# 18 of 22 feature tiles of each SwiGLU input projection in pairs through seven block products, with buffer pools opened and closed per sublayer

## The chip, the core and the metric

The kernel runs on one core of one Trainium2 chip. TensorE (PE) does the matmuls and writes to PSUM; VectorE (DVE), ScalarE (ACT) and GpSimd (POOL) do the elementwise work; each engine runs its own queue in program order and waits on semaphores. SyncE (SP) issues nearly all DMAs, in one queue. The metric is the device time of one execution in microseconds; lower is better. One execution was also profiled, and every row below is from that one.

## The reference: four layers of mixer and SwiGLU

There are 512 tokens of 1024 features in float32. Four layers each hold a token mixer (mLSTM, sliding-window attention, HGRN2, differential attention, in that order) and a SwiGLU channel mixer. Both are modulated by a conditioning vector and followed by a residual sum and a layer norm:

```python
FFN_HIDDEN = -(-8 * D_MODEL // (3 * 256)) * 256      # 2816
...
def swiglu(h, w_in, w_out):
    gu = h @ w_in
    return (jax.nn.silu(gu[..., :FFN_HIDDEN]) * gu[..., FFN_HIDDEN:]) @ w_out
...
    mod = jnp.einsum('bd,sde->sbe', cond, ada_w[i].astype(F32)) + ada_b[i][:, None, :].astype(F32)
    shift, scale, gate = jnp.split(mod.astype(x.dtype), 3, axis=-1)
...
    h = x * (1 + scale[1][:, None]) + shift[1][:, None]
    y = swiglu(h, ffn_w_in[i], ffn_w_out[i])
    x = layer_norm(DEEPNORM_ALPHA * x + (1 + gate[1][:, None]) * y.astype(x.dtype), ln_g[i, 1], ln_b[i, 1])
```

## The kernel before

Activations lie features by tokens: 128 partitions, 8 feature tiles (KD), 512 tokens. Every large matmul is done as three: both operands are split into a high part and a remainder, and `mm3` (L187 to L191) adds high x high (L189), low x high (L190) and high x low (L191) in PSUM. For the weights, `weights` (L170 to L185) loads a tile of up to 128 x 1024 into a `raw` buffer by DMA, ACT copies it to `wh` (L179), and DVE takes `wl` = raw - wh (L180). `raw` and `wp` (the pool of wh and wl) have five buffers each, so splits run ahead of PE by that much. The activations' high and low parts are `hh` (L424, ACT) and `hl` (L428, DVE, which subtracts hh from the POOL result `h` of L427); `modulate` makes the three per feature tile and token half.

The SwiGLU (`ffn`, L431 to L457) has 22 hidden feature tiles, each with a gate and an up projection: 8 k-tiles x 3 matmuls of 512 columns for each of the two, 48 a tile. The first two tiles run in two halves of 256 tokens, since the layer norm ahead delivers its halves one after the other. `gated` makes the activation of a tile: silu on ACT (L441), product on DVE (L442), the high copy on ACT (L443), the low part on DVE (L444). Tiles come in groups of 7, 7 and 8 (FGROUPS); after each group `out_proj` (L307 to L358) multiplies them into the 8 output rows and adds each to the residual (L326). In a sublayer's last group, rows 4 to 7 run in two token halves, A and B: layer norm (L361 to L411) of half 0 and its modulation run beside half B, and the next sublayer's input projection starts on half 0 when half B has been multiplied. The layer norm's rsqrt is a power on POOL (L487, `lnv`).

The conditioning (`ada`) is a matrix-vector product done by DVE: 24 columns for each of the 8 sublayers, 192 in all, each a load of 512 KB and one DVE instruction of 128x1024 (L113, with a short second row). They are kept in a list `todo`; each `weights` call pops `rate` of them.

Buffers: `big` (12) and `mid` (10) are pools for all sublayers, opened once in `__init__` (L47 to L57). A mixer's first buffers can therefore be written while the SwiGLU ahead still runs. Three such early writes matter here: the zeroed buffer of the sliding-window mixer (L700, POOL), the seven masks of HGRN (L944 to L949, five POOL instructions for each), and a load of the differential mixer's vectors on ACT's queue (L812). The order of the instructions comes from Python generators that `run` (L1128 to L1177) advances, and from a scheduler that places each instruction in its engine's queue by priority and readiness.

Of the kernel before, what the change touches and what calls it, by code (L numbers as in the profile page):

```python
# [19 lines left out]
P = 128  # L20
D = 1024
T = 512
KD = D // P
NTT = T // P
DEPTH = 4
HID = 2816
KF = HID // P
FGROUPS = (7, 7, 8)
# [13 lines left out]
class Trunk:  # L42
    rate, hold = 1, 0

    def __init__(self, ctx, tc, a, out):
        self.tc, self.nc, self.a, self.out = tc, tc.nc, a, out
        pool = lambda name, bufs, **k: ctx.enter_context(tc.tile_pool(name=name, bufs=bufs, **k))  # L47
        self.const = pool("const", 1)
        self.state = pool("state", 1)
        self.raw = pool("raw", 5)  # L50
        self.wp = pool("wp", 5)
        self.big = pool("big", 12)
        self.mid = pool("mid", 10)
# [63 lines left out]
    def ada_begin(self, sub, js=range(24)):  # L117
        mod = self.adap.tile([P, 24], F32, tag="mod", name=self.nm("mod"), bufs=3)
        self.todo += [lambda j=j: self.ada_column(mod, sub, j) for j in js]
# [21 lines left out]
    def first_input(self, sub, gate):
        nc, gp, V = self.nc, self.nc.gpsimd, self.nc.vector
        mod = self.ada_begin(sub, ())
# [22 lines left out]
        self.todo += [lambda j=j: self.ada_column(mod, sub, j) for j in range(16, 24)]  # L166
        self.todo.append(lambda: gp.tensor_scalar(gate, mod[:, 16:24], 1.0, None, ALU.add))
# [193 lines left out]
    def layer_norm(self, sub, nxt, half):  # L361
        nc = self.nc
        V = nc.vector
        t = slice(half * 256, half * 256 + 256)

        ps = self.bank()
# [6 lines left out]
        s, v = (self.lnp.tile([P, 2], F32, tag=x, name=self.nm(x), bufs=2) for x in ("lns", "lnv"))  # L373
# [47 lines left out]
    def modulate(self, z, hs, hb, k, t, eng=None):  # L421
        nc = self.nc
        h = self.lnp.tile([P, T], F32, tag="h", name=self.nm("h"), bufs=2)[:, t]
# [6 lines left out]

    def ffn(self, layer, gate):  # L431
        nc, a = self.nc, self.a
        j0 = 0
        for gi, gn in enumerate(FGROUPS):
            acts = []

            def gated(pss):
                for pg, pu in zip(pss[::2], pss[1::2]):
                    act = self.b4([P, 2, T], F32R)
                    s = self.b2([P, T])  # L440
                    nc.scalar.activation(s, pg, AF.Silu)  # L441
                    nc.vector.tensor_tensor(s, pu, s, ALU.mult)  # L442
                    nc.scalar.activation(act[:, 0, :], s, AF.Copy)  # L443
                    nc.vector.tensor_tensor(act[:, 1, :], s, act[:, 0, :].bitcast(F32), ALU.subtract)  # L444
                    acts.append(act)

            j = j0
            while j < j0 + gn:
                m = 2 if (gi == 0 and j == 0) else 1
                srcs = [a["ffn_in"][layer, jj, :, x, :] for jj in range(j, j + m) for x in range(2)]  # L450
                yield from self.proj_cols(srcs, "t" if m == 2 else None, gated)
                j += m
            srcs = [a["ffn_out"][layer, d, :, j0 * P : (j0 + gn) * P] for d in range(KD)]
            if gi == len(FGROUPS) - 1:
                return srcs, 1, acts
            yield from self.out_proj(srcs, 1, acts, gate, False)
            j0 += gn  # L457
# [670 lines left out]
    def run(self, plan):  # L1128

        self.setup()  # L1130
        subs = [2 * l + (k == "ffn") for k, l in plan]
# [3 lines left out]
        for i, (kind, layer) in enumerate(plan):  # L1135
            more = i + 1 < len(plan)
            gate = mods[2] if i else gate
            gen = getattr(self, kind)(layer, gate)
# [10 lines left out]
            self.rate, self.hold = 2 if kind == "mlstm" else 1, 10 if kind == "ffn" else 0  # L1149
# [27 lines left out]
        self.run_all(ln)  # L1177

# [14 lines left out]
def host(inputs):  # L1193
# [10 lines left out]
    r["ffn_in"] = w.transpose(0, 4, 2, 3, 1, 5).reshape(DEPTH, KF, P, 2, D)  # L1204
# [63 lines left out]
```

## Time and profile before

| what | us |
|---|---|
| timed runs, median (lowest to highest of 3) | 2482.39 (2480.66 to 2485.26) |
| the profiled execution's own time | 2479.98 |
| its span, first to last instruction | 2478.0 |
| PE busy in the span | 2434.8 |
| DVE / ACT / POOL busy | 1427.7 / 917.0 / 469.2 |

The four SwiGLU sublayers take some 360 us each. A matmul's record is longer than the distance to the next one, since matmuls are pipelined; the start-to-start distance is what a matmul costs in a full stream. A row of the views reads: line of the kernel, engine, operation, output <- inputs by the program's names, partitions x elements, and count; then busy time and mean duration, and the idle time before, with what ended it.

### The profile page before, as it was taken

What the parts mean: (1) busy time and instruction counts of PE and PEld (TensorE: products, weight loads), DVE (VectorE), ACT (ScalarE), POOL (GpSimd) and SP (SyncE); (2) the same over time, 40 slices, a digit from 0 to 9 for tenths busy, and PEclk for the clock granted to TensorE, in tenths of its full rate; (3) what the DMA queues carried; (4) which work ended last, traced back from release to release, by engine and by line L of the source; (5) the groups of instructions that cost most, each with busy time, mean ns of one, the idle gap of its engine ahead of it and who ended that gap; (6) DMA issues with size and microseconds to landing.
All of it is one profiled execution on the core that took longest, in us unless ns stands there. A gap on an engine that the chain in (4) does not pass through costs nothing.

```text
span 2478.0 us, 34314 instructions
## 1 busy us (share of the span) xinstructions
PE 2434.8 (98%) x12920; PEld 2054.2 (83%) x12920; DVE 1427.7 (58%) x2745; ACT 917.0 (37%) x1685; POOL 469.2 (19%) x714
## 2 busy tenths in 40 slices
PE   7999999999999999999999999999999999999998
PEld 5778888888768888889888898888888888888887
DVE  6956765545687656546555576565365557433334
ACT  3534422233654422234433344222345554422223
POOL 5003100003334000105333340000052124000002
PEclk9999999999999999999999999999999999999999
DMA  8842466642211566632212215666322211333331
GB/s 299 282 150 78 152 215 188 199 147 69 77 52 52 187 204 196 203 111 69 86 60 69 70 60 188 203 199 201 113 67 86 66 57 48 104 102 93 102 94 35
DMA packets 93973, 311.94 MB, mean 126 GB/s; under 512 B 10736, under 2 KB 13168, under 8 KB 93808
## 3 DMA queue, kind: packets, MB, share of 16 engines
q1 hardware_dynamic: 92800, 309.43, 39.0%
q8 instruction: 101, 1.65, 0.3%
q14 instruction: 64, 0.52, 0.1%
q10 hardware_dynamic: 1008, 0.32, 0.1%
HBM read 307.62 MB, written 2.10 MB: 125 GB/s over the span
## 4 chain that ended last, share of the span: by engine, by line
PE 87%; DVE 7%; POOL 2%; ACT 1%; issue 1%; DMA 1%; ACTq 0%; POOLq 0%; DVEq 0%
PE ps L189 26%; PE ps L191 26%; PE ps L190 26%; DVE wl L180 1%; PE ps L876 1%; PE ps L1042 1%; DVE raw L113 1%; POOL h L427 1%; PE ps L738 1%; PE ps L1103 1%; PE ps L904 1%; DVE xz L394 1%; PE ps L769 1%; DVE xz L402 1%; DMA raw<-in_m_vo 1%
## 5 line engine op out<-in xcount | busy, mean ns | idle before, releaser
L179 ACT ACTIVATE wh<-raw 128x1024 fp32r<-128x1024 f32 (+1 forms) x395 | 410.7, 1043 | 1011.2 <-PE ps L190 607.1
L189 PE MATMUL ps<-hh,wh 128*128 128x512 f32 (+1 forms) x1768 | 655.6, 372 | 16.2 <-ACT wh L179 13.1
L191 PE MATMUL ps<-hh,wl 128*128 128x512 f32 (+1 forms) x1768 | 657.5, 372 | 3.0 <-DVE wl L180 2.9
L190 PE MATMUL ps<-hl,wh 128*128 128x512 f32 (+1 forms) x1768 | 656.0, 372 | 0.4
L180 DVE TENSOR_TENSOR wl<-raw,wh 128x1024 fp32r<-128x1024 f32 (+1 forms) x395 | 492.9, 1251 | 273.8 <-ACT wh L179 251.3
L189 PE MATMUL ps<-b,wh 128*128 128x512 f32 (+1 forms) x1216 | 425.9, 351 | 0.0
L190 PE MATMUL ps<-b,wh 128*128 128x512 f32 (+1 forms) x1216 | 419.2, 345 | 0.0
L191 PE MATMUL ps<-b,wl 128*128 128x512 f32 (+1 forms) x1216 | 418.9, 345 | 0.0
L189 PEld LDWEIGHTS ps<-hh,wh 128*128 128x128 f32 x1768 | 333.3, 189 | 73.0 <-ACT wh L179 13.1
L191 PEld LDWEIGHTS ps<-hh,wl 128*128 128x128 f32 x1768 | 334.1, 189 | 63.4 <-DVE wl L180 6.4
L190 PEld LDWEIGHTS ps<-hl,wh 128*128 128x128 f32 x1768 | 334.0, 189 | 58.9 <-DVE hl L428 1.3
L113 DVE CUSTOM_DVE_ANT_0 raw<-raw,cond,adab 128x1024 f32<-128x1024 f32 x192 | 247.9, 1296 | 216.4 <-DMA raw<-in_ada_w 216.3
L189 PEld LDWEIGHTS ps<-b,wh 128*128 128x128 f32 x1216 | 230.3, 189 | 29.5 <-issue 1.2
L190 PEld LDWEIGHTS ps<-b,wh 128*128 128x128 f32 x1216 | 230.4, 189 | 29.3 <-issue 2.0
L191 PEld LDWEIGHTS ps<-b,wl 128*128 128x128 f32 x1216 | 230.2, 189 | 27.7
L189 PE MATMUL ps<-wh,hh 128*128 128x512 f32 (+1 forms) x608 | 239.3, 395 | 2.2 <-ACT wh L179 1.2
L326 DVE SCALAR_TENSOR_TENSOR xz<-ps,gate,xz 128x512 f32<-128x512 f32 (+1 forms) x208 | 130.0, 626 | 181.2 <-PE ps L191 180.6
L190 PE MATMUL ps<-wl,hh 128*128 128x512 f32 (+1 forms) x608 | 221.4, 364 | 0.1
L191 PE MATMUL ps<-wh,hl 128*128 128x512 f32 (+1 forms) x608 | 221.3, 364 | 0.0
L442 DVE TENSOR_TENSOR b<-ps,b 128x512 f32<-128x512 f32 x88 | 60.3, 690 | 138.3 <-PE ps L191 135.5
L189 PEld LDWEIGHTS ps<-wh,hh 128*128 128x128 f32 x608 | 115.1, 189 | 23.1 <-issue 3.7
L190 PEld LDWEIGHTS ps<-wl,hh 128*128 128x128 f32 x608 | 115.0, 189 | 18.3 <-issue 2.2
(254 smaller groups left out, 2376.8 us busy)
## 6 DMA issues: line engine op xcount, KB each, us to landing
raw<-in_ada_w SPq DMA_DIRECT2D x192, 512.0 KB, 4.0
raw<-in_ffn_in SPq DMA_DIRECT2D x176, 512.0 KB, 3.7
raw<-in_ffn_out SPq DMA_DIRECT2D x64, 448.0 KB, 3.5
raw<-in_ffn_out SPq DMA_DIRECT2D x32, 512.0 KB, 3.6
raw<-in_m_vo SPq DMA_DIRECT2D x16, 512.0 KB, 4.9
raw<-in_h_qf SPq DMA_DIRECT2D x16, 512.0 KB, 3.3
raw<-in_h_ig SPq DMA_DIRECT2D x16, 512.0 KB, 3.9
raw<-in_d_qk SPq DMA_DIRECT2D x16, 512.0 KB, 3.9
```

Source lines behind the costliest of these rows:

```text
L113: self.nc.vector.tensor_tensor_reduce(w, w, self.cond, 1.0, self.adab[:, sub, j : j + 1], ALU.mult, ALU.add, mod[:, j : j + 1])
L179: nc.scalar.activation(hi[:, :n], raw[:, :n], AF.Copy)
L180: (eng or nc.vector).tensor_tensor(lo[:, :n], raw[:, :n], hi[:, :n].bitcast(F32), ALU.subtract)
L189: nc.tensor.matmul(ps, lhs[0], rhs[0], start=start, stop=False)
L190: nc.tensor.matmul(ps, lhs[0], rhs[1], start=False, stop=False)
L191: nc.tensor.matmul(ps, lhs[1], rhs[0], start=False, stop=stop)
L326: nc.vector.scalar_tensor_tensor(z, ps[:, t], gate[:, d : d + 1], z, ALU.mult, ALU.add)
L394: V.tensor_tensor(z, z, st[:, 0, :], ALU.subtract)
L402: V.tensor_tensor(z, z, st[:, 1, :], ALU.mult)
L427: nc.gpsimd.tensor_scalar(h, z, hs[:, k : k + 1], hb[:, k : k + 1], ALU.mult, ALU.add)
L442: nc.vector.tensor_tensor(s, pu, s, ALU.mult)
L738: nc.tensor.matmul(ps, qTs[j][:, q], kz[:, :, k0 : k0 + nk * P], start=True, stop=True)
```

## The change

**Seven products.** Tiles 0 to 3 stay as they were. The other 18 tiles go in nine pairs a layer. For a pair, the weights form a 2 x 2 block matrix (gate and up; input features 0 to 511 and 512 to 1023; a block is two feature tiles of 128 by four k-tiles, 128 x 1024 in memory), and the activations form another (the two halves of the features; tokens 0 to 255 and 256 to 511). `strassen` forms the 2 x 2 product with seven block products instead of eight. A product is 2 x 4 x 3 = 24 matmuls of 256 columns; a pair has 168 of them, where there were 96 of 512 columns. The combinations of activation blocks (`t_forms`) are made and split once a layer, from the `h` tiles, which are now kept (`keep`) in four raw buffers until then. The combinations of weight blocks are made for each pair: DVE adds R3 += R2, R0 += R3, R3 = R0 - R2 and R1 += R0 in place, and each is split into high and low like any weight, so a pair has seven splits (four before) and four weight sums. Partial results are summed in PSUM banks and in ACT's copies of them. The next pair's first products are issued between the last ones of a pair.

**Order around it.** FGROUPS becomes (8, 8, 6). `rate` is 0 in the SwiGLU's input part, 2 in its first two output projections and 1 in the last; `hold` is 0. `ada_end` forces only the columns of its own sublayer.

**Pools.** `raw` gets seven buffers. `big`, `mid`, and the SwiGLU's `tf`, `pairs` and `mid` are opened at the start of each sublayer and closed at its end, in the same memory.

```diff
-FGROUPS = (7, 7, 8)
+FGROUPS = (8, 8, 6)
+FPLAIN = 4
...
+    def pools(self, kind):
+        if self.own:
+            self.own.close()
+        self.own = ExitStack()
+        pool = lambda name, bufs: self.own.enter_context(self.tc.tile_pool(name=self.nm(name), bufs=bufs))
+        if kind == "ffn":
+            self.tf, self.pairs, self.mid = pool("tf", 4), pool("pairs", 4), pool("mid", 7)
+        else:
+            self.big, self.mid = pool("big", 12), pool("mid", 10)
...
+    def t_forms(self):
+        nc, V = self.nc, self.nc.vector
+        b11, b12, b21, b22 = (self.keep[x] for x in ((0, 0), (0, 1), (1, 0), (1, 1)))
+        V.tensor_tensor(b11, b11, b12, ALU.subtract)
+        V.tensor_tensor(b12, b22, b12, ALU.subtract)
+        V.scalar_tensor_tensor(b22, b11, -1.0, b22, ALU.mult, ALU.subtract)
+        V.scalar_tensor_tensor(b21, b22, -1.0, b21, ALU.mult, ALU.subtract)
...
+        for i, r in ((6, b22), (5, b11), (7, b12), (4, b21)):
+            f = self.tf.tile([P, 2, 4, 256], F32R, tag="tf", name=self.nm("tf"))
+            nc.scalar.activation(f[:, 0], r, AF.Copy)
+            V.tensor_tensor(f[:, 1], r, f[:, 0].bitcast(F32), ALU.subtract)
+            forms[i] = [f[:, 0], f[:, 1]]
...
+        def product(ps, w, i, first):
+            for j in range(2):
+                for k in range(4):
+                    c = slice(j * 512 + k * P, j * 512 + k * P + P)
+                    m = [x[:, k, :] for x in forms[i]]
+                    for a, b in ((0, 0), (0, 1), (1, 0)):
+                        nc.tensor.matmul(
+                            ps[:, j * 256 : j * 256 + 256],
+                            w[a][:, c],
+                            m[b],
...
+        product(b2, w, 1, True)
+        p1 = copy(b2)
...
+        product(b1, w, 2, True)
+        add(p1, b1, p1)
+        nc.scalar.activation(p1, p1, AF.Silu)
+        yield
+        load(2)
+        load(3)
+        add(R[3], R[3], R[2])
+        add(R[0], R[0], R[3])
+        w = self.split(R[0])
+        product(b2, w, 6, False)
+        u2 = copy(b2)
+        yield
+        w = self.split(R[3])
+        b3 = self.bank()
+        product(b3, w, 5, True)
+        yield
+        V.tensor_tensor(R[3], R[0], R[2], ALU.subtract)
+        w = self.split(R[3])
+        product(b2, w, 7, False)
+        u3 = copy(b2)
+        add(u3, b3, u3)
+        yield
+        w = self.split(R[2])
+        product(b2, w, 4, False)
...
+        gated(0, p1, b2)
+        yield
+        add(R[1], R[1], R[0])
+        w = self.split(R[1])
+        product(b3, w, 3, False)
+        add(u2, b3, u2)
+        nc.scalar.activation(u2, u2, AF.Silu)
+        gated(1, u2, u3)
+        yield
...
+        for i in range(n):
+            g, act = steps[i]
+            for s in range(5):
+                if s == 3:
+                    begin(i + 1)
+                if s == 4 and i + 1 < n:
+                    next(steps[i + 1][0])
+                next(g)
+                yield 0.0
```

How the queues move is seen at three places. The first is DVE in the middle of a SwiGLU's input part. Before, a tile's rows and two columns of the conditioning alternate (`b` is an activation buffer, `wl` the weights' low part):

```order
L442 TENSOR_TENSOR b_402_2456<-ps_2406,b_402_2456 128x512 [waits PE_49]
L113 ISA raw_2612,mod_2086<-raw_2612,cond,adab 128x1024 [waits DMAHW7_49,DVE_49]
L113 ISA mod_2086 128x1
L444 TENSOR_TENSOR b_401_2455<-b_402_2456,b_401_2455 128x512 [waits Activation_49]
L180 TENSOR_TENSOR wl_2600<-raw_2597,wh_2599 128x1024 [waits DMAHW4_49]
L113 ISA raw_2677,mod_2086<-raw_2677,cond,adab 128x1024 [waits DMAHW1_49]
L113 ISA mod_2086 128x1
L180 TENSOR_TENSOR wl_2609<-raw_2606,wh_2608 128x1024 [waits DMAHW6_49,PE_49,Activation_49]
```

With the change, about half of one pair's rows in the same queue (L516 are sums of weights or of PSUM with a buffer, L480 splits, L542 the difference R0 - R2, L554 the gated product, L556 its low part):

```order
L480 TENSOR_TENSOR wl_3797<-raw_3533,wh_3796 128x1024 [waits PE_49,Activation_49]
L480 TENSOR_TENSOR wl_3836<-raw_3698,wh_3835 128x1024 [waits PE_49,Activation_49]
L516 TENSOR_TENSOR b_551_3694<-ps_3640,b_551_3694 128x512 [waits Activation_49]
L480 TENSOR_TENSOR wl_3866<-raw_3831,wh_3865 128x1024 [waits PE_49,Activation_49]
L542 TENSOR_TENSOR raw_3831<-raw_3698,raw_3829 128x1024 [waits DVE_49]
L554 SCALAR_TENSOR_TENSOR b_532_3500<-ps_3475,b_532_3500 128x512 [waits PE_49]
L480 TENSOR_TENSOR wl_3896<-raw_3831,wh_3895 128x1024 [waits Activation_49]
L556 TENSOR_TENSOR pair_3468<-b_532_3500,pair_3468 128x2x256 [waits Activation_49]
L516 TENSOR_TENSOR b_557_3729<-ps_3768,b_557_3729 128x512 [waits PE_49]
L480 TENSOR_TENSOR wl_3930<-raw_3927,wh_3929 128x1024 [waits DMAHW6_49,Activation_49]
L516 TENSOR_TENSOR raw_4060<-raw_4060,raw_4058 128x1024 [waits DMAHW1_49,DMAHW0_49]
```

The columns of the conditioning are gone from this part; in their place stand weight sums and more splits, between rows that wait for PE.

The second place is DVE at the end of a group, in the change: the last pair's sums and products, then the output projection's weights (L191) and the conditioning (L124).

```order
L191 TENSOR_TENSOR wl_4366<-raw_4363,wh_4365 128x1024 [waits DMAHW2_49]
L516 TENSOR_TENSOR b_607_4187<-ps_4226,b_607_4187 128x512 [waits PE_49]
L191 TENSOR_TENSOR wl_4404<-raw_4401,wh_4403 128x1024 [waits DMAHW5_49,Activation_49]
L124 ISA raw_4407,mod_2091<-raw_4407,cond,adab 128x1024 [waits DMAHW6_49]
L124 ISA mod_2091 128x1
L516 TENSOR_TENSOR b_595_4092<-ps_4098,b_595_4092 128x512 [waits PE_49]
L124 ISA raw_4410,mod_2091<-raw_4410,cond,adab 128x1024 [waits DMAHW7_49]
L124 ISA mod_2091 128x1
L554 SCALAR_TENSOR_TENSOR b_595_4092<-b_601_4152,b_595_4092 128x512 [waits Activation_49]
```

Between u2's sum after product 3 (the second L516) and the rows that turn it into an activation stand columns that wait for their own loads; before the change there were no such sums.

The third place is POOL at the passage from the second SwiGLU to HGRN. Before, the masks' rows (L944 to L949) stood far ahead, inside the SwiGLU, and at the passage the modulation's rows (L427) followed one another:

```order
L427 TENSOR_SCALAR h_9551<-xz,hs_9177,hb_9178 128x256 [waits DVE_49]
L427 TENSOR_SCALAR h_9587<-xz,hs_9177,hb_9178 128x256 [waits DVE_49]
L337 TENSOR_TENSOR S<-S,sq_9581 128x256 [waits Activation_49]
L427 TENSOR_SCALAR h_9593<-xz,hs_9177,hb_9178 128x256 [waits DVE_49,Pool_49]
L427 TENSOR_SCALAR h_9599<-xz,hs_9177,hb_9178 128x256 [waits DVE_49]
```

With the change (L447 is the modulation, L1111 to L1116 the masks):

```order
L447 TENSOR_SCALAR h_11200<-xz,hs_10862,hb_10863 128x256 [waits DVE_49]
L1111 MEMSET b_1658_11302 128x128 [waits PE_49]
L348 TENSOR_TENSOR S<-S,sq_11224 128x256 [waits Activation_49]
L1112 MEMSET b_1658_11302 128x64 [waits Pool_49]
L1111 MEMSET b_1659_11308 128x128
L1114 AFFINE_SELECT b_1658_11302<-b_1658_11302 128x128 [waits Pool_49]
L1112 MEMSET b_1659_11308 128x32x2 [waits Pool_49]
L1111 MEMSET b_1660_11314 128x128
L1115 AFFINE_SELECT b_1658_11302<-b_1658_11302 128x128 [waits Pool_49]
L1114 AFFINE_SELECT b_1659_11308<-b_1659_11308 128x128 [waits Pool_49]
L1116 CAST hmasks<-b_1658_11302 128x128 [waits Pool_49]
L1115 AFFINE_SELECT b_1659_11308<-b_1659_11308 128x128 [waits Pool_49]
```

The masks now stand between the first and the second modulation row, and the first of them waits for PE: for the last matmul of the output projection's half B, which releases the SwiGLU's pools. The remaining masks lie between the other modulation rows of half 0.

More of the change, by code (lines that the diff above doesn't have):

```diff
@@ L42 @@
 class Trunk:
-    rate, hold = 1, 0
+    rate, hold, keep = 1, 0, None
     def __init__(self, ctx, tc, a, out):
@@ L57, in __init__ @@
         self.ps = pool("ps", 8, space=PSUM)
+        self.raw = pool("raw", 7)
+        self.wp = pool("wp", 5)
+        self.own = None
         self.todo = []
@@ L117, in ada_begin @@
     def ada_begin(self, sub, js=range(24)):
[L118 to L119 removed]
+        mod = self.adap.tile([P, 32], F32, tag="mod", name=self.nm("mod"), bufs=3)
+        self.todo += [(sub, lambda j=j: self.ada_column(mod, sub, j)) for j in js]
         return mod
@@ L165, in first_input @@
             gp.tensor_scalar(z, z, ALPHA, 0.0, ALU.mult, ALU.add)
-        self.todo += [lambda j=j: self.ada_column(mod, sub, j) for j in range(16, 24)]
-        self.todo.append(lambda: gp.tensor_scalar(gate, mod[:, 16:24], 1.0, None, ALU.add))
+        self.todo += [(sub, lambda j=j: self.ada_column(mod, sub, j)) for j in range(16, 24)]
+        self.todo.append((sub, lambda: gp.tensor_scalar(gate, mod[:, 16:24], 1.0, None, ALU.add)))
     def weights(self, src, n, eng=None):
@@ L372, in layer_norm @@
                 )
-        s, v = (self.lnp.tile([P, 2], F32, tag=x, name=self.nm(x), bufs=2) for x in ("lns", "lnv"))
+        s, v = (
+            self.lnp.tile([P, w], F32, tag=x, name=self.nm(x), bufs=2)[:, :2] for x, w in (("lns", 38), ("lnv", 2))
+        )
         V.tensor_scalar(s, ps[:, 0:2], 1.0 / D, None, ALU.mult)
@@ L422, in modulate @@
         nc = self.nc
-        h = self.lnp.tile([P, T], F32, tag="h", name=self.nm("h"), bufs=2)[:, t]
+        if self.keep is None:
+            h = self.lnp.tile([P, T], F32, tag="h", name=self.nm("h"), bufs=2)[:, t]
+        else:
+            x = (k // 4, t.start // 256)
+            if x not in self.keep:
+                self.keep[x] = self.raw.tile([P, 4, 256], F32, tag="raw", name=self.nm("H"))
+            h = self.keep[x][:, k % 4, :]
         nc.scalar.activation(
@@ L431, in ffn @@
     def ffn(self, layer, gate):
         nc, a = self.nc, self.a
[L433 to L457, printed above, removed]
@@ new lines, in gated @@
+        def gated(tile, j, pg, pu):
+            act = tile[:, :, j, :]
+            s = self.b2([P, T])
+            nc.scalar.activation(s, pg, AF.Silu)
+            nc.vector.tensor_tensor(s, pu, s, ALU.mult)
+            nc.scalar.activation(act[:, 0, :], s, AF.Copy)
+            nc.vector.tensor_tensor(act[:, 1, :], s, act[:, 0, :].bitcast(F32), ALU.subtract)
+        self.rate = 0
+        acts = []
+        src = lambda j: [a["ffn_in"][layer, j, :, x, :] for x in range(2)]
+        pa, pb = self.pair_tile(), self.pair_tile()
@@ new lines, in ffn, with begin @@
+        yield from self.proj_cols(
+            src(0) + src(1), "t", lambda ps: (gated(pa, 0, ps[0], ps[1]), gated(pa, 1, ps[2], ps[3]))
+        )
+        yield from self.proj_cols(src(2), None, lambda ps: gated(pb, 0, *ps))
+        forms = self.t_forms()
+        yield from self.proj_cols(src(3), None, lambda ps: gated(pb, 1, *ps))
+        for x in (pa, pb):
+            acts += [x[:, :, 0, :], x[:, :, 1, :]]
+        n = (KF - FPLAIN) // 2
+        steps = [None] * n
+        def begin(i):
+            if i < n:
+                act = self.pair_tile()
+                steps[i] = self.strassen(a["ffn_dp"][layer, i], forms, act), act
+                next(steps[i][0])
@@ new lines, in ffn @@
+        ends, j0 = np.cumsum(FGROUPS), 0
+        begin(0)
+        next(steps[0][0])
+        for i in range(n):
[7 more added lines that the diff above has]
+                yield 0.0
+            acts += [act[:, :, 0, :], act[:, :, 1, :]]
+            gn = len(acts)
+            if j0 + gn in ends:
+                srcs = [a["ffn_out"][layer, d, :, j0 * P : (j0 + gn) * P] for d in range(KD)]
+                self.rate = 2
+                if j0 + gn == KF:
+                    self.rate = 1
+                    return srcs, 1, acts
+                yield from self.out_proj(srcs, 1, acts, gate, False)
+                self.rate = 0
+                acts = []
+                j0 += gn
@@ L1148, in run @@
                         begun[x] = self.ada_begin(x)
-            self.rate, self.hold = 2 if kind == "mlstm" else 1, 10 if kind == "ffn" else 0
+            self.rate, self.hold = 2 if kind == "mlstm" else 1, 0
             if i > 0:
@@ L1164, in run @@
             if more:
-                mods = self.ada_end(begun[n], self.lng[:, s, :], self.lnb[:, s, :])
+                mods = self.ada_end(n, begun[n], self.lng[:, s, :], self.lnb[:, s, :])
             nxt = mods[:2] if more else None
+            self.keep = {} if more and plan[i + 1][0] == "ffn" else None
             out = self.out_proj(srcs, per, acts, gate, True)
@@ L1177, in run @@
         self.run_all(ln)
+        self.own.close()
     def advance(self, gen, n):
```

59 lines of the change are left out of this document (51 added, 8 removed).

## The prediction

> **What bounds the kernel now.** I read the page's shares first, then its chain of waits.
>
> ```profile
> PE 2434.8 (98%) x12920; PEld 2054.2 (83%) x12920; DVE 1427.7 (58%) x2745; ACT 917.0 (37%) x1685; POOL 469.2 (19%) x714
> ...
> PE 87%; DVE 7%; POOL 2%; ACT 1%; issue 1%; DMA 1%; ACTq 0%; POOLq 0%; DVEq 0%
> ```
>
> TensorE (PE) is busy 98% of the span and holds 87% of the chain that ended last. The list of PE's waits shows what is left.
>
> ```profile
> PE ps L189 <- ACT wh L179: 14.3, 2, 13.1
> PE ps L189 <- ACT hh L424: 4.1, 6, 0.8
> PE ps L191 <- DVE wl L180: 2.9, 9, 0.5
> ```
>
> The 14.3 us are the kernel's start; the rest is small. So time goes only with PE work, and any other edit can only add waits. The table by stage, for the insides of the first and the last SwiGLU (columns: window, its length, then busy time and count of PE, PEld, DVE, ACT, POOL; granted clock, DMA share, GB/s):
>
> ```profile
> 270.00:600.00 330.00, 330.00 (x1515) 275.72 (x1515) 186.15 (x241) 94.77 (x119) 20.29 (x23) 1.00 0.56 176
> ...
> 2125.00:2450.00 325.00, 325.00 (x1479) 271.01 (x1479) 121.08 (x129) 90.04 (x113) 14.56 (x13) 1.00 0.29 91
> ```
>
> PE doesn't idle there; DVE has 144 of 330 us free, ACT 235. What one matmul costs is its start-to-start pace, not the 0.39 or 0.28 us of its record, which overlaps the next ones. From PE's timeline:
>
> ```profile
> 419.63 0.39 PE L190 MATMUL ps<-hl,wh 128*128 128x512 f32 x1
> ...
> 432.32 0.39 PE L189 MATMUL ps<-hh,wh 128*128 128x512 f32 x1
> ...
> 590.15 0.28 PE L189 MATMUL ps<-b,wh 128*128 128x256 f32 x1
> ...
> 602.03 0.28 PE L189 MATMUL ps<-b,wh 128*128 128x256 f32 x1
> ```
>
> Between the first two lie 56 steps: 12.69/56 = **226.6 ns** for 512 columns. Between the others lie 99: 11.88/99 = **120.0 ns** for 256. A half-width matmul costs 53%, not 50%: 13.4 ns of each are fixed.
>
> **The matmuls.** A pair of tiles (gate and up, two tiles each) took 4 x 24 = 96 matmuls of 512 columns, 96 x 0.2266 = 21.75 us. Seven products of 24 matmuls of 256 are 168 x 0.1200 = 20.16 us. The saving is 1.59 us a pair, and over 36 pairs **-57.4 us**. By count alone (one product of eight, 12.5%) it would be 36 x 21.75/8 = -97.9; the fixed part eats 40 of them.
>
> The Trainium skill, "TensorE: Matmul & The Clock Gate", section "Back-to-back issue gap", gives a warm gap of N/2.4 + 2.5 ns; worked out from that, an estimate is 109 and 216 ns and -86 us for the 36 pairs. The two paces above, each some 11 ns longer than the formula, contradict it; the sum goes by them, and that side is a rival below.
>
> The groups of the output projection go from 7, 7, 8 to 8, 8, 6. Half of the last group's rows run in two halves, so two tiles of 3 x 4 matmuls each go from 2 x 0.1200 back to 0.2266: 24 x 0.0134 = 0.3 us a layer, **-1.3** in all.
>
> **What DVE and ACT get.** Groups of the first SwiGLU's window by shape (count, then busy us, mean ns of one, idle before):
>
> ```profile
> L180 DVE TENSOR_TENSOR wl<-raw,wh 128x1024 fp32r<-128x1024 f32 x48 | 62.4, 1302 | 34.6 <-ACT wh L179 33.8
> L113 DVE CUSTOM_DVE_ANT_0 raw<-raw,cond,adab 128x1024 f32<-128x1024 f32 x48 | 61.6, 1284 | 56.0 <-DMA raw<-in_ada_w 56.0
> ...
> L442 DVE TENSOR_TENSOR b<-ps,b 128x512 f32<-128x512 f32 x22 | 15.1, 690 | 26.4 <-PE ps L191 25.8 <-ACT b L441 0.7
> L326 DVE SCALAR_TENSOR_TENSOR xz<-ps,gate,xz 128x512 f32<-128x512 f32 x20 | 15.0, 750 | 14.5 <-PE ps L191 14.3
> L444 DVE TENSOR_TENSOR b<-b,b 128x512 fp32r<-128x512 f32 x22 | 15.0, 685 | 0.0
> ...
> L179 ACT ACTIVATE wh<-raw 128x1024 fp32r<-128x1024 f32 x48 | 50.9, 1062 | 157.2 <-PE ps L190 101.6 <-issue 49.5 <-PE ps L191 5.3
> ...
> L443 ACT ACTIVATE b<-b 128x512 fp32r<-128x512 f32 x22 | 13.8, 631 | 8.7 <-DVE b L442 8.6
> L441 ACT ACTIVATE b<-ps 128x512 f32<-128x512 f32 x22 | 12.7, 582 | 0.0
> ```
>
> A pair now needs on DVE 7 weight splits and 4 weight sums of 128x1024, 5 operations of 128x512 that read PSUM and 2 splits of 128x512: 11 x 1.302 + 5 x 0.690 + 2 x 0.685 = 19.1 us at full record length. Back to back, such records overlap too:
>
> ```profile
> 1160.23 1.22 DVE L180 TENSOR_TENSOR wl<-raw,wh 128x1024 fp32r<-128x1024 f32 x1
> 1161.36 0.15 DVE L374 TENSOR_SCALAR lns<-ps 128x2 f32<-128x2 f32 x1
> ```
>
> The next one starts 1.13 us after the split, so the pair takes about 11 x 1.13 + 5 x 0.69 + 2 x 0.6 = 17.1 us. Both are under PE's 20.16, by 1.1 and by 3.1 us. ACT has 7 x 1.06 + 3 x 0.58 + 2 x 0.58 + 2 x 0.63 = 11.6 us. That fits because the ada columns (1.284 us each on L113) no longer run in the input part (rate 0); they move to the output projections, where DVE needs per feature row 1.3 + 2 x 1.28 + 0.75 = 4.6 us against 24 x 0.2266 = 5.4 on PE. So the steady state is PE-bound on average. It isn't free of stalls: DVE works in program order, and behind a sum that waits for PE's bank stand the splits of later products; product 7 adds into the bank that ACT has just copied as u2. Five weight buffers let splits run four products (11.5 us) ahead, which covers most of it. Bounds: 0, and 0.8 us a pair (one ACT copy of 0.58 with a handover), 29 us. I take 0.15 a pair, nearer to 0 as waits for splits cost 2.9 us in all now: **+5**.
>
> The token combinations (t_forms) put 4 sums and 4 splits of 128x1024 on DVE, 8 x 1.13 = 9 us a layer, and 4 copies on ACT, beside tiles 2 and 3 (2 x 48 x 0.2266 = 21.8 us of PE): 0. Weight loads are four of 512 KB per 20 us, as before; a load lands in 3.7 us:
>
> ```profile
> raw<-in_ffn_in SPq DMA_DIRECT2D x176, 512.0 KB, 3.7
> ```
>
> **Group ends.** At the 12 ends of groups the last pair has no following pair to fill PE. After product 3 run u2's sum, silu, product, ACT copy and split: 0.69 + 0.58 + 0.69 + 0.63 + 0.69 = 3.3 us, with one to three ada columns of 1.28 queued between them on DVE, since the rate is 2 by then: 4.6 to 7.1 us. PE has the other tiles of the first output row meanwhile, 23 matmuls, 5.2 us. So 0 to 1.9 us each, 0 to 23 in all, and no pair of the old kernel shows it; I take 0.5 each, **+6**.
>
> **Pools.** The SwiGLU and mixer buffers now share memory, and the first buffer of a new mixer waits until the last half-row of the output projection has been multiplied. Before, three things ran ahead, under PE. One is HGRN's masks, on POOL inside the second SwiGLU (window 1030 to 1080, by shape):
>
> ```profile
> L947 POOL TENSOR_SCALAR_AFFINE_SELECT b<-b 128x128 f32<-128x128 f32 x7 | 4.7, 665 | 0.0
> L948 POOL TENSOR_SCALAR_AFFINE_SELECT b<-b 128x128 f32<-128x128 f32 x7 | 4.5, 650 | 0.0
> L949 POOL CAST hmasks<-b 128x128 uint8<-128x128 f32 x7 | 2.0, 290 | 0.1
> L944 POOL MEMSET b<- 128x128 f32 x5 | 1.0, 206 | 48.6 <-DVE b L444 48.6
> L945 POOL MEMSET b<- 128x64 f32 x6 | 0.8, 154 | 0.0
> ```
>
> That is 13.0 us (a few memsets missing from the records). After the change these 35 instructions stand in POOL's queue among the eight modulate steps (h) of half 0, behind a wait for that last matmul. What it looked like before:
>
> ```profile
> 1148.64 0.56 POOL L427 TENSOR_SCALAR h<-xz,hs,hb 128x256 f32<-128x256 f32 x1 [0.34 <-DVE xz L402]
> ...
> 1152.67 0.28 PE L189 MATMUL ps<-hh,wh 128*128 128x256 f32 x1
> ...
> 1163.27 0.73 POOL L487 TENSOR_TENSOR lnv<-lnv,mhalf 128x2 f32<-128x2 f32 x1 [3.42 <-DVE lnv L377]
> ...
> 1166.26 0.60 ACT L424 ACTIVATE hh<-xz,hb,hs 128x256 fp32r<-128x256 f32 x1 [8.04 <-DVE xz L402]
> ...
> PE ps L384 <- POOL lnv L487: 0.4, 1, 0.4
> PE ps L370 <- DVE S L336: 0.3, 1, 0.3
> PE ps L191 <- DVE wl L180: 0.2, 1, 0.2
> ```
>
> The h steps ran from 1148.6, PE went at 1152.67 (call it B) from the output projection into HGRN's input projection, and the three waits in 1135 to 1185 are 0.9 us together. Now only h of k=0 is early; k=1 comes after two masks, about B+7.5, k=3 near B+13.6, k=7 near B+18 (13.0 of masks and seven h of 0.56). PE takes the feature tiles in that order, 12 x 0.120 = 1.44 us each, so it ends half 0 near B+21 rather than B+12.7. POOL's lnv of half 1, now behind all h, and the normalisation and modulation behind it (1163.27 to the first hh at 1166.26 before, longer now with splits and ada columns between) hold half 1 back to about B+26. That is 13 us against B+12.7; the bounds are 8 (half 0 alone) and 17 (all masks and h steps, no overlap): **+13**.
>
> The sliding-window mixer's zeroed buffer does the same on POOL, once:
>
> ```profile
> 480.00 0.96 POOL L700 MEMSET b<- 128x1024 f32 x1
> ```
>
> It moves between h of k=0 and k=1, and half B itself, 6 tiles rather than 8, covers 2.9 us less (72 rather than 96 matmuls of 0.120). 0 to 5, taken **+2**. In the differential mixer it is the load of lv on ACT's queue, ahead of later hh steps: the same 2.9 us and its issue, 0 to 6, taken **+2.5**. At the kernel's end nothing follows: 0. The 8 ada columns that spill into each mixer (10 us of DVE, 42% idle over the span) I cost at 0; uncovered, they'd be part of the two bounds above.
>
> **The sum.** The profiled execution lasted 2479.98 us (span 2478.0 and 2.0 around it). 2480.0 - 57.4 - 1.3 + 5 + 6 + 13 + 2 + 2.5 = 2449.8. The median of the timed runs, 2482.39, lies 2.4 higher, so I forecast **2452**.
>
> **Rivals.**
> - DVE becomes the bound of a pair. For it: 19.1 of 20.16 us by record length, in-order waits for PSUM, dependent sums (R3, then R0) that can't overlap. Against: 17.1 by pace, and four products of lookahead. Price: PE's gain is 58.7, the other terms cost 23.5, so from 35.2/36 = 0.98 us more a pair (21.1 us) the kernel is slower than before. At a typical 22 us a pair: 36 x 1.84 = 66 in place of 5, **2513**. Chance 0.11.
> - The 256-wide stream is held by weight loads. For it, their records:
>
> ```profile
> L189 PEld LDWEIGHTS ps<-hh,wh 128*128 128x128 f32 x1768 | 333.3, 189 | 73.0 <-ACT wh L179 13.1
> ```
>
> At 189 ns a matmul a pair takes 168 x 0.189 = 31.8 us, +361 in place of -57: about 2870. From 129.5 ns on it eats the whole gain. The 99 steps at 120.0 say that loads overlap. Chance 0.01.
> - The fixed 13.4 ns vanish in the product stream (the side of the skill's formula): -97.9 instead of -57.4, 2412. Against it, the same 99 steps. Chance 0.01.
> - The boundaries are dearer, all terms near their upper ends (15 + 20 + 17 + 5 + 6 - 28.5 = 34 more): 2486, no change. Chance 0.07.
> - The waits come out near their lower bounds (steady state, group ends, sliding-window and differential mixer 0, masks 8): 5 + 6 + 2 + 2.5 + 5 = 20 less, 2432. Chance 0.13; still faster.
> - The change doing something else than it says: the count of matmuls is fixed by the code; below 0.01.
>
> My forecast, the waits as summed, has 0.67. The range takes the forecast's own 2438 to 2470, the cheap case and the dear one: **2430 to 2486**; DVE's rival lies outside. A measurement of this kernel tells about 0.2% (5 us) from no change: faster, below 2477, has 0.81, within 0.07, slower 0.12.
>
> **What would show it.** Right: PE steps of 120 ns in the product lines, about 20.2 us a pair, PE waiting less than 10 us there; masks on POOL just behind the second SwiGLU with a PE idle of some 13 us; small PE waits for DVE at group ends. Wrong: PE waiting for DVE splits in every pair (first rival), a pace other than 120 ns, or no idle time at HGRN's start.

## The result, and the profile after

The change makes the kernel slower: 2518.29 us median (2511.04 to 2520.41, 4 runs) against 2483.2 for the kernel before (2480.66 to 2485.26, 4 runs). The ratio is 1.0137, 95% interval 1.0113 to 1.016. The forecast was 2452 with a range of 2430 to 2486, so even the sign was wrong. One run of a kernel below, masks_out, was in a slower state (2594.63 us at a granted clock of 0.875) and is left out of its median.

The page of the profiled execution (span 2517.9 us), first part and chain of waits:

```profile
PE 2407.0 (96%) x15416; PEld 2148.6 (85%) x15416; DVE 1811.3 (72%) x3137; ACT 1104.9 (44%) x1917; POOL 476.9 (19%) x714
...
PE 73%; DVE 13%; DMA 6%; issue 3%; POOL 2%; ACT 2%; ACTq 0%; DVEq 0%; POOLq 0%; SPq 0%
...
PE ps L502 18%; PE ps L200 15%; PE ps L202 15%; PE ps L201 15%; DMA raw<-in_ada_w 4%; DVE raw L124 3%; DVE wl L191 3%; DVE wl L480 2%; PE ps L1209 1%; PE ps L1043 1%; PE ps L905 1%; ACT wh L190 1%; PE ps L1270 1%; PE ps L1071 1%; DVE xz L408 1%
```

PE has 28 us less work recorded, and the span is 40 us longer. The chain, 87% PE before, is 73% PE; DVE has 13% of it where it had 7, and the loads of the conditioning (`in_ada_w`), which were not among its listed lines, hold 4%. PE's waits (total, times, longest):

```profile
PE ps L200 <- ACT wh L190: 38.8, 6, 13.1
PE ps L200 <- ACT pair L555: 22.4, 9, 3.5
PE ps L381 <- DVE S L347: 10.9, 5, 2.7
PE ps L201 <- DVE hl L448: 6.3, 2, 4.8
PE ps L200 <- ACT hh L444: 5.9, 4, 2.2
...
PE ps L502 <- ACT b L513: 0.5, 1, 0.5
```

Line L502, the seven products, waited 0.5 us in the whole kernel. So the new arithmetic runs as it should, and the time goes elsewhere: to the start of the SwiGLUs (wh, 13.1 of its 38.8 being the kernel's start), to group ends (pair) and to the boundaries (S, hl, hh). The inside of the last SwiGLU, by windows (columns as in the prediction):

```profile
2300.00:2320.00 20.00, 20.00 (x169) 20.00 (x168) 17.06 (x18) 11.03 (x15) 0.00 (x0) 1.00 0.36 106
```

A pair, 168 matmuls, passes in some 20 us at 0.12 us each, and DVE is busy for 17.06 us of these 20, with the 18 rows of one pair. Both were forecast: 20.16 and 17.1.

**Where the time went, by sublayer.** A sublayer is measured from the last matmul of one sublayer's final output projection to the next such matmul. For the last SwiGLU, before and then after:

```profile
2094.97 0.28 PE L191 MATMUL ps<-b,wl 128*128 128x256 f32 x1
...
2463.44 0.28 PE L191 MATMUL ps<-b,wl 128*128 128x256 f32 x1
```

```profile
2140.60 0.28 PE L202 MATMUL ps<-b,wl 128*128 128x256 f32 x1
...
2502.61 0.28 PE L202 MATMUL ps<-pair,wl 128*128 128x256 f32 x1
```

These are 368.5 and 362.0 us. The same for all sublayers and for the kernels that follow, in us (each from one profiled execution):

| kernel | mLSTM | SwiGLU 1 | sliding w. | SwiGLU 2 | HGRN | SwiGLU 3 | diff. | SwiGLU 4 | end |
|---|---|---|---|---|---|---|---|---|---|
| before | 244.9 | 368.5 | 170.6 | 368.5 | 312.0 | 368.7 | 261.7 | 368.5 | 14.6 |
| after | 243.3 | 376.4 | 175.5 | 378.2 | 325.6 | 374.4 | 267.2 | 362.0 | 15.3 |
| early_w | 243.4 | 366.7 | 175.6 | 371.2 | 325.4 | 370.6 | 267.4 | 354.8 | 15.3 |
| masks_out | 244.1 | 373.8 | 175.5 | 377.9 | 314.5 | 377.8 | 267.0 | 361.1 | 16.1 |
| no_load | 243.5 | 365.8 | 175.0 | 368.5 | 323.9 | 366.2 | 266.1 | 362.0 | 15.3 |
| no_ada | 244.8 | 355.8 | 174.3 | 355.8 | 313.5 | 356.1 | 264.0 | 354.8 | 15.3 |
| g868 | 243.5 | 366.8 | 173.6 | 362.5 | 322.1 | 367.2 | 264.4 | 355.0 | 14.6 |
| fix | 244.2 | 364.9 | 177.7 | 365.0 | 317.8 | 364.4 | 267.1 | 354.8 | 15.6 |
| fix2 | 244.0 | 359.5 | 178.2 | 360.7 | 318.3 | 359.0 | 267.0 | 354.9 | 15.6 |
| best | 244.1 | 358.3 | 178.2 | 357.7 | 318.6 | 358.4 | 265.6 | 355.2 | 14.7 |
| two_cols | 244.1 | 361.3 | 179.0 | 362.8 | 317.5 | 360.1 | 266.0 | 355.1 | 14.6 |

SwiGLU 4 gains 6.5 us, the other three lose 6 to 10. It is the only one with no columns of the conditioning to compute, as no sublayer follows it: a control inside the same run. In the kernel before, where the first three have these columns too, all four take 368.5 to 368.7 us.

**The SwiGLU's start.** PE's timeline and ACT's, after:

```profile
243.32 0.28 PE L202 MATMUL ps<-b,wl 128*128 128x256 f32 x1
249.72 0.58 PE L200 MATMUL ps<-hh,wh 128*128 128x256 f32 x1 [6.12 <-ACT wh L190]
...
247.32 1.09 ACT L444 ACTIVATE hh<-xz,hb,hs 128x256 fp32r<-128x256 f32 x2 [1.02 <-DVE xz L416]
...
248.62 1.04 ACT L190 ACTIVATE wh<-raw 128x1024 fp32r<-128x1024 f32 x1
```

ACT's copy of the first weight tile stands behind seven of the eight hh rows of half 0, and each of those waits for DVE's layer norm. In the kernel before, this copy came in between:

```profile
234.56 1.06 ACT L179 ACTIVATE wh<-raw 128x1024 fp32r<-128x1024 f32 x1 [0.38 <-PE ps L190]
```

The tile itself had long landed: the first four loads were issued before 207 us. Only the place in ACT's queue is late. The wait is 6.1 us at each of the four starts.

**The end of a group.** DVE and ACT at the end of the first SwiGLU's last group, after:

```profile
574.49 1.29 DVE L124 CUSTOM_DVE_ANT_0 raw<-raw,cond,adab 128x1024 f32<-128x1024 f32 x1 [0.86 <-DMA raw<-in_ada_w]
...
577.14 1.28 DVE L124 CUSTOM_DVE_ANT_0 raw<-raw,cond,adab 128x1024 f32<-128x1024 f32 x1 [1.35 <-DMA raw<-in_ada_w]
...
578.35 0.68 DVE L554 SCALAR_TENSOR_TENSOR b<-ps,b 128x512 f32<-128x512 f32 x1
...
579.07 0.63 ACT L555 ACTIVATE pair<-b 128x512 fp32r<-128x512 f32 x1 [2.81 <-DVE b L554]
...
583.29 0.50 PE L200 MATMUL ps<-pair,wh 128*128 128x512 f32 x1 [1.54 <-ACT pair L555]
```

DVE waits for the load of a column, then computes it, twice, before it comes to the gated product (L554) of the last pair; ACT and PE wait down the line. PE's own row at the end of that sublayer's first group shows how long the first output row covers for it:

```profile
346.12 0.28 PE L502 MATMUL ps<-hh,wl 128*128 128x256 f32 x1
...
352.86 0.50 PE L200 MATMUL ps<-pair,wh 128*128 128x512 f32 x1 [2.12 <-ACT pair L555]
```

Between the two rows stand 19 matmuls of 512 columns, 18 of them for the six tiles of this row that were ready, 4.3 us in all; in a last group, of six tiles, there are 15, 3.4 us. PE waits for `pair` at each of the nine group ends of the first three SwiGLUs, 1.5 to 3.5 us each and 22.4 us in all, and at none of the fourth, where no columns stand in between.

**HGRN's masks.** POOL and PE at the passage from the second SwiGLU, after:

```profile
1172.95 0.56 POOL L447 TENSOR_SCALAR h<-xz,hs,hb 128x256 f32<-128x256 f32 x1 [1.72 <-DVE xz L416]
1173.73 0.21 POOL L1111 MEMSET b<- 128x128 f32 x1 [0.22 <-PE ps L202]
...
1180.20 0.56 POOL L447 TENSOR_SCALAR h<-xz,hs,hb 128x256 f32<-128x256 f32 x1
...
1181.33 0.58 PE L201 MATMUL ps<-hl,wh 128*128 128x256 f32 x1 [4.77 <-DVE hl L448]
...
1188.36 0.36 POOL L1116 CAST hmasks<-b 128x128 uint8<-128x128 f32 x1
...
1197.11 0.72 POOL L654 TENSOR_TENSOR lnv<-lnv,mhalf 128x2 f32<-128x2 f32 x1
```

With B = 1173.5, h of k=1 comes at B+6.7 (forecast B+7.5), the last mask at B+15, and HGRN takes 13.6 us more. This passage went as forecast.

### The profile page after: what moved, and what is told of

Same layout as the page of the kernel before. It is cut to its first block, busy times and chain, and to the rows that moved or that the text cites. A ratio compares the mean times of both kernels' runs of the same rounds, so it can differ in the third digit from the quotient of the medians.

```text
span 2517.9 us, 39980 instructions
## 1 busy us (share of the span) xinstructions
PE 2407.0 (96%) x15416; PEld 2148.6 (85%) x15416; DVE 1811.3 (72%) x3137; ACT 1104.9 (44%) x1917; POOL 476.9 (19%) x714
## 4 chain that ended last, share of the span: by engine, by line
PE 73%; DVE 13%; DMA 6%; issue 3%; POOL 2%; ACT 2%; ACTq 0%; DVEq 0%; POOLq 0%; SPq 0%
PE ps L502 18%; PE ps L200 15%; PE ps L202 15%; PE ps L201 15%; DMA raw<-in_ada_w 4%; DVE raw L124 3%; DVE wl L191 3%; DVE wl L480 2%; PE ps L1209 1%; PE ps L1043 1%; PE ps L905 1%; ACT wh L190 1%; PE ps L1270 1%; PE ps L1071 1%; DVE xz L408 1%
## 5 line engine op out<-in xcount | busy, mean ns | idle before, releaser
L479 ACT ACTIVATE wh<-raw 128x1024 fp32r<-128x1024 f32 x252 | 267.0, 1061 | 424.3 <-PE ps L502 161.6
L502 PE MATMUL ps<-tf,wh 128*128 128x256 f32 x2304 | 418.3, 283 | 0.5 <-ACT b L513 0.5
L480 DVE TENSOR_TENSOR wl<-raw,wh 128x1024 fp32r<-128x1024 f32 x252 | 307.6, 1223 | 110.7 <-ACT wh L479 110.6
L191 DVE TENSOR_TENSOR wl<-raw,wh 128x1024 fp32r<-128x1024 f32 (+1 forms) x251 | 302.5, 1212 | 110.2 <-ACT wh L190 92.0
L502 PEld LDWEIGHTS ps<-tf,wh 128*128 128x128 f32 x2304 | 359.8, 192 | 2.9 <-ACT b L513 2.3
L502 PE MATMUL ps<-tf,wl 128*128 128x256 f32 x1152 | 326.0, 283 | 0.0
L200 PE MATMUL ps<-pair,wh 128*128 128x512 f32 (+1 forms) x800 | 295.1, 370 | 22.4 <-ACT pair L555 22.4
L201 PE MATMUL ps<-pair,wh 128*128 128x512 f32 (+1 forms) x800 | 294.1, 369 | 0.0
L202 PE MATMUL ps<-pair,wl 128*128 128x512 f32 (+1 forms) x800 | 293.3, 368 | 0.0
L124 DVE CUSTOM_DVE_ANT_0 raw<-raw,cond,adab 128x1024 f32<-128x1024 f32 x192 | 255.7, 1344 | 48.6 <-DMA raw<-in_ada_w 48.5
L502 PE MATMUL ps<-hh,wl 128*128 128x256 f32 x864 | 244.5, 283 | 0.0
L502 PE MATMUL ps<-hl,wh 128*128 128x256 f32 x864 | 244.5, 283 | 0.0
L502 PE MATMUL ps<-hh,wh 128*128 128x256 f32 x864 | 244.5, 283 | 0.0
L502 PEld LDWEIGHTS ps<-tf,wl 128*128 128x128 f32 x1152 | 221.1, 192 | 0.0
```

The costliest lines, as they stand in the source:

```text
L124: self.nc.vector.tensor_tensor_reduce(w, w, self.cond, 1.0, self.adab[:, sub, j : j + 1], ALU.mult, ALU.add, mod[:, j : j + 1])
L191: (eng or nc.vector).tensor_tensor(lo[:, :n], raw[:, :n], hi[:, :n].bitcast(F32), ALU.subtract)
L200: nc.tensor.matmul(ps, lhs[0], rhs[0], start=start, stop=False)
L201: nc.tensor.matmul(ps, lhs[0], rhs[1], start=False, stop=False)
L202: nc.tensor.matmul(ps, lhs[1], rhs[0], start=False, stop=stop)
L479: nc.scalar.activation(hi, raw, AF.Copy)
```

## The experiments

All ratios are to the kernel before the change, run on the same chip in the same call. The changed kernel ran in the first call alone; differences of medians to it, as given below for the first three kernels, come out 3 to 4 us larger than the ratios have them. Each edit is shown against the changed kernel, or against the kernel on top of which it is made.

**early_w: the first four weight tiles ahead of the kept H buffers.** In the changed kernel `modulate` takes the kept `H` tiles from the `raw` pool, so in its order of buffers the next SwiGLU's first loads come behind H tiles that are first written during the layer norm.

```diff
+            if self.keep is not None:
+                rate, self.rate = self.rate, 0
...
+                self.pre = [self.weights(x, D) for x in first]
+                self.rate = rate
             ln = self.layer_norm(subs[i], nxt, 0)
...
     def weights(self, src, n, eng=None):
+        if self.pre:
+            return self.pre.pop(0)
```

> Theory: the kept H buffers stand in the raw rotation, so ACT's copies of the next SwiGLU's first four weight tiles are queued behind layer norm's hh rows, and PE waits 6.1 us at each of the four SwiGLU starts. This kernel loads and splits those four tiles just after half A, ahead of the H buffers; nothing else changes. Expected: the four 6.1 us waits for wh gone, about 25 us off, 2493. Rival: the layer norm itself (hh, hl) or the split's wl sets that start anyway, and the wait only changes its name: 8 us off at most, 2510 or more.

Measured: 2490.36 us, 28 less than the changed kernel; ratio 1.0038 (1.0023 to 1.0053). The 6.1 us waits are gone from PE's list, which leaves the kernel's own start and little else under that name, and ACT's copy stands again where it stood before the change:

```profile
PE ps L202 <- ACT pair L557: 19.6, 9, 3.2
PE ps L202 <- ACT wh L192: 14.3, 2, 13.1
```

```profile
233.05 1.06 ACT L192 ACTIVATE wh<-raw 128x1024 fp32r<-128x1024 f32 x1 [0.38 <-PE ps L203]
```

SwiGLU 4 falls from 362.0 to 354.8. That is 13.7 us under the kernel before, and it is what the seven products bring where little disturbs them. The edit moves the loads, the splits and their place among the buffers together. So it shows what the late copies cost; that the H tiles in `raw` are what made them late is read from the order of the buffers in the code, and no run gave these tiles a pool of their own.

**masks_out: a buffer of their own for the masks.**

```diff
+        self.msk = pool("msk", 1)
...
-            m = self.b2([P, nb, 2, h])
+            m = self.msk.tile([P, nb, 2, h], F32, tag="m", name=self.nm("m"))
```

> Theory: HGRN is 13.6 us longer because its masks wait for the SwiGLU's pools and stand among POOL's modulation rows. This kernel gives the masks a buffer of their own that is open from the start. Expected: masks run far ahead, HGRN's stretch falls from 325.5 to about 312, 13 us off, 2505. Rival: half 0 at HGRN's start is held by the conditioning's columns and the shorter half B, not by the masks: 3 us off at most, 2515.

Measured: 2507.56 us, 11 less than the changed kernel where 13 were forecast; ratio 1.011 (1.0093 to 1.0126). HGRN falls from 325.6 to 314.5, 11.1 us; PE's wait for hl, 6.3 us before, is no longer among its larger ones. The remaining 2.5 us of the 13.6 have another cause.

**no_load: the conditioning without its loads.**

```diff
-        self.nc.sync.dma_start(w, self.a["ada_w"][sub, j])
+        if sub < 2:
+            self.nc.sync.dma_start(w, self.a["ada_w"][sub, j])
         self.nc.vector.tensor_tensor_reduce(
-            w, w, self.cond,
+            w, w if sub < 2 else self.cond, self.cond,
```

> Leaves out the loads of the conditioning's weights for sublayers 2 to 7 (the DVE instruction stays, and multiplies the condition with itself). Theory: the first three SwiGLUs are some 14 us longer than the fourth, which has no columns, because DVE waits for a column's load while the last pair's activation rows stand behind it. Expected: the first three fall from 368 to 372 us to about 357, the pair waits of PE at the ends of groups go, and with the mixers' starts 40 to 48 us come off: 2474. Rival: it is the DVE time of the columns (1.3 us each), not their loads: 10 us off at most, 2508 or more.

Measured: 2488.79 us, ratio 1.0032 (1.0019 to 1.0045), 29.5 less than the changed kernel; forecast were 40 to 48 less. The first three SwiGLUs fall by 10.6, 9.7 and 8.2. PE's waits within 300 to 600 us, in the changed kernel and then without the loads:

```profile
PE ps L200 <- ACT pair L555: 7.2, 3, 3.5
```

```profile
PE ps L382 <- DVE S L348: 2.4, 1, 2.4
```

The waits for the pair's activation are gone. But these SwiGLUs are still 3.8 to 6.5 us longer than the fourth, which has the same start, so loads are about two thirds of the columns' cost, and not all of it. The edit also takes 144 loads of 512 KB out of the one load queue, so that other loads may come sooner; that it acts by DVE's waits is read from DVE's rows above. PE's lists name no load as what ended a wait, with these loads or without, but the two ways were not separated by a run.

**no_ada: no columns at all,** on top of early_w and masks_out.

```diff
     def ada_column(self, mod, sub, j):
+        if sub >= 2:
+            self.nc.gpsimd.memset(mod[:, j : j + 1], 0.0)
+            return
```

> Early weights and masks of their own, and the 144 columns of the conditioning for sublayers 2 to 7 left out altogether (loads and DVE work; their modulation becomes zero). Theory: the columns cost the first three SwiGLUs what separates them from the fourth, partly by loads (28.6 us, as the kernel without loads showed), partly by DVE time; without them each takes the 354.8 us of the fourth, so the early-weights kernel's 2490 loses 44 and the masks' 11: 2435. Rival: something else that only the first three have, the modulation of the mixer behind them and its pools, costs 3 to 5 us in each: 2447.

Measured: 2436.2 us, as expected (2435); ratio 0.982 (0.9805 to 0.9834). All four SwiGLUs are now alike, 354.8 to 356.1. So the columns, DVE time and loads together, are nearly the whole of what separates the first three from the fourth. The mixers don't come back with them: without any columns the sliding-window mixer still takes 174.3 us, HGRN 313.5 and the differential one 264.0, which is 3.7, 1.5 and 2.3 more than before the change.

**g868: groups (8, 6, 8),** on top of early_w.

```diff
-FGROUPS = (8, 8, 6)
+FGROUPS = (8, 6, 8)
```

> Early weights, and the groups (8, 6, 8) instead of (8, 8, 6). Theory: half B of a last group of 6 covers 2.9 us less of the layer norm, which is part of the 5 us that the sliding-window and the differential mixers lose; with 8 they come back by 2.9 us each, HGRN by 0 to 3, less 1.3 us in all for the halves: 2490 to 2483. Rival: those mixers wait for buffers of the closed pools, and half B's length doesn't matter: 2491.

Measured: 2474.09 us (2470.52 to 2480.8), ratio 0.9971 (0.9961 to 0.998): 16 us less than early_w, twice the best that was expected. In the profiled executions, which lie 20.8 us apart, the sliding-window mixer gains 2.0, the differential one 3.0 and HGRN 3.3. Another 8.7 and 3.4 us come from SwiGLU 2 and 3, which no theory here had; the last projection gives each row 8 tiles of PE time rather than 6 beside one column, which would fit, but that was not tested by itself. That column stands in the last projection here too, so the mixers' gain need not be the length of half B alone; the kernel best below, without it, shows less.

**fix: early_w, masks_out, and columns spread.**

```diff
-                self.rate = 2
+                self.rate = 1
...
                 next(g)
+                if s in (1,):
+                    self.ada_steps(1)
                 yield 0.0
```

> Early weights and masks of their own as in the two kernels before, and the conditioning spread: one column for each pair and rate 1 instead of 2 in the first two output projections, the rest in the following mixer. Theory: 25 and 13 us off as above, and 10 to 25 more as fewer columns stand ahead of the last pair: 2455 to 2470, faster than the kernel before the change. Rival: the columns among a pair's rows make DVE the bound there (17.1 + 1.3 of 20.0 us) or stall it on loads, and what is won at group ends is lost: 2480 or more.

Measured: 2473.43 us, ratio 0.9969 (0.9958 to 0.998), a little short of what was expected: by the table, of the loss by columns about a third is gone, and HGRN and the sliding-window mixer, which got more columns, give 3 and 2 us back.

**fix2: columns kept off the first rows of a projection,** on top of fix.

```diff
-                self.rate = 1
+                self.rate, self.hold = 2, 3
...
-                    self.rate = 1
+                    self.rate, self.hold = 0, 0
                     return srcs, 1, acts
```

> As the kernel with early weights, masks and spread columns (2473), but no columns with the first three weight tiles of the middle output projections (then 2 each) and none in the last one; 19 columns are left to each mixer. Theory: what is left of the loss at group ends (PE waits of 7 us for the pair's activation and 12 for the layer norm's sums) comes from columns that stand ahead of these rows: 10 to 14 us off, 2460. Rival: the columns that move into the mixers cost as much there: 2470 or more.

Measured: 2458.71 us, as the theory had it; ratio 0.991 (0.9895 to 0.9925). The first three SwiGLUs are at 359 to 361, 14.5 us together above the fourth, where early_w had 44.1 and fix 29.9.

**best and two_cols: fix2 with groups (8, 6, 8), and the same with two columns a pair and rate 1 in the middle projections.**

```diff
-                if s in (1,):
+                if s in (1, 3):
                     self.ada_steps(1)
...
-                self.rate, self.hold = 2, 3
+                self.rate, self.hold = 1, 3
```

> The two best edits together: early weights, masks of their own, spread columns kept off the first rows of the output projections, and the groups (8, 6, 8). Theory: the gains add up, since the groups act on the mixers' starts (2 to 3 us each) and the columns on the ends of groups; with no columns in the last projection the groups' extra gain in the SwiGLUs is gone: 2459 - 8 = 2451. Rival: both had removed the same waits: 2457 or more.

> As the kernel before it in this call, with two columns for each pair rather than one and rate 1 in the middle projections. Theory of the prediction's first rival: a pair's DVE work is 17.1 us by pace, so 17.1 + 2 x 1.29 = 19.7 of PE's 20.0 is still under the bound on average, but with no room for in-order waits: each pair of the first three SwiGLUs loses 0.3 to 1.5 us, 27 pairs: 10 to 40 us slower than the other. If DVE has more room than that, within 4 us of the other.

Measured: best 2453.14 us (2452.18 to 2455.66), ratio 0.9885 (0.987 to 0.9899), 1.2% faster than the kernel before and the fastest here that computes everything; two_cols 2460.98, ratio 0.9911 (0.9894 to 0.9928). The groups add only 5.6 us to fix2, and not where the theory had them: the sliding-window mixer and HGRN stay as they were (178.2, and 318.3 to 318.6), the differential one gains 1.4, and the first three SwiGLUs gain 1.2, 3.0 and 0.6. With no columns in the last projection, and 19 in each mixer, the longer half B gave those two mixers nothing. The kernel two_cols is 8 us slower than best (1.7 to 5.1 in each of the first three SwiGLUs of the profiled executions), which is between the two outcomes that were written down, 10 to 40 and at most 4. It changes the columns of a pair and the rate in the middle projections together. More of PE's waits there are for `pair`, as at the group ends of the other kernels:

```profile
PE ps L203 <- ACT pair L558: 7.6, 7, 1.7
```

The same wait is 3.1 us in best, and the line of the products stands in neither list at all.

## Why the prediction was wrong

- **The matmuls: right, slightly large.** The pace of 120.0 ns a half-width matmul held, and with it the saving of 14.7 us a layer (57.4 + 1.3 over four). SwiGLU 4 in early_w shows 13.7. Both rivals about the pace fall; the second was priced at -97.9, where the estimate that it went back to gives -86.
- **DVE as the bound of a pair: not so.** The sum of 17.1 us was right, the products wait 0.5 us in all, and the +5 for the steady state was not needed. Even with two columns in each pair (two_cols) the products wait nowhere. The measured time lies next to this rival's 2513 by chance; its mechanism did not occur.
- **The step that failed first: the kept h tiles, costed at 0.** The prediction counted t_forms' operations, found PE work to hide them under, and never asked what four more buffers in the `raw` rotation do to the order of the queues. The moved instruction was not one of t_forms but ACT's copy of the next SwiGLU's first weights. PE's four waits are 6.1 us each, and early_w, which moves the copies back, gains 28 us by the medians and 25 by the ratios. Why the copies moved is the part that no run isolates.
- **The step that failed second: group ends, +6 taken from bounds of 0 to 23.** The mechanism was named, columns queued between the last pair's rows, but priced as DVE time of one to three columns; a column also waits for its load on DVE, in program order. The prediction's own row for L113 had that price: 56.0 us of idle time for loads over 48 columns, nearly as much as the 61.6 of their work. The cover was too long as well: 23 matmuls, 5.2 us, leave out one matmul of the row, but the last pair is two of its tiles, and PE had 19 (4.3 us), or 15 (3.4 us) in a group of six. So PE waited 22.4 us for `pair` at nine group ends. With the waits at the layer norm behind the last projection, the first three SwiGLUs lose 14.4, 16.2 and 12.4 us against the fourth, 43 in all. no_load takes 28.5 of them, and no_ada leaves 3.3 of the 44.1 that early_w has. The remark that the columns fit in the projections, 4.6 of 5.4 us a row, was an average that left the loads out.
- **The pools: right for HGRN, low for the other two.** HGRN +13 forecast, 13.6 measured, 11.1 of them shown to be the masks. The sliding-window and differential mixers lose 4.9 and 5.5 where 2 and 2.5 were taken within 0 to 5 and 0 to 6. Without columns they still lose 3.7 and 2.3, so columns are only part of it. The groups gave 2 and 3 back in g868 and 0 and 1.4 in best, so half B's 2.9 us in these terms is neither shown nor excluded; that their early writes wait for the pools was not tried alone.

In one line, by sublayers of the table: -54.8 for products and groups (4 x 13.7), +28.8 for the starts (4 x 7.2, 362.0 less 354.8, taken to be the same at all four), +43.0 for the columns, +24.0 in the mixers, -0.9 at the two ends: +40.1, where the spans differ by 39.9.

## What to carry to other kernels

A saving on the engine that is the bound is worth what the queues of the others let through: before costing one, look in the order of the instructions for every row that now stands ahead of the first work of the next stage, not only for rows that were added. A buffer that is held for longer in a rotating pool can change the order of whatever shares that pool. Work put into a stage because an engine has time there on average should still stay away from the rows on which the bound engine will wait, and a row that itself waits for a load was the dearest of them here.

## What the runs showed of the hardware

Idle time of PE can cost more than itself. After the 2.72 us for S at 608.69 in the changed kernel, matmuls of 256 columns follow at 0.21 us instead of 0.12 for more than 3 us:

```profile
608.69 1.87 PE L381 MATMUL ps<-ones,S 128*128 128x1 f32 x8 [2.72 <-DVE S L347]
610.42 0.56 PE L200 MATMUL ps<-pair,wh 128*128 128x256 f32 x1
...
613.34 0.41 PE L201 MATMUL ps<-pair,wh 128*128 128x256 f32 x1
613.55 0.41 PE L202 MATMUL ps<-pair,wl 128*128 128x256 f32 x1
```

The granted clock of 240 to 260 us, where the wait of 6.1 us falls, is 0.74, and the mean of the whole kernel 0.981, against 0.997 before and in best:

```profile
240.00:260.00 20.00, 13.21 (x86) 12.49 (x85) 15.28 (x36) 9.35 (x15) 8.69 (x11) 0.74 0.23 72
```

Not every wait does it: the one of 2.12 us at 352.86 is followed by the full pace, and so are those of 2.79 us at 1138.20 and 2.87 us at 1838.22, while the slow steps come within some 1 us behind those of 3.03 us at 907.69 and 3.52 us at 480.87. At 608.69 the eight matmuls of one column behind the wait count too: no matmul of 256 or 512 columns ran for some 4.4 us. The Trainium skill ("TensorE: Matmul & The Clock Gate", section "What's actually happening") tells of a gate that halves the clock after an idle window of some 3.4 us that runs free of the program; these stretches lie on both sides of that figure and agree with it roughly, with the recorded wait of 3.03 us below it. Counted in the traces, steps of 0.20 to 0.225 us for 256 columns and 0.41 to 0.44 for 512, with no recorded wait, add 50 us over the full pace in the changed kernel and 34 in the kernel before; by that estimate (some matmul records are missing) the slow steps are 16 us of what was lost, and PE's recorded waits, 101 us in all against 33, the kernel's start included, are most of it.
